# A decode step with staged caches: other landing estimates, one more staging buffer, and dependencies counted in the prompt's softmax

## The chip, the core and the metric

The kernel runs on one core of a Trainium2 chip. Five engines run their own instruction streams in program order: TensorE (PE in the profile, its weight loads PEld), VectorE (DVE), ScalarE (ACT), GpSimd (POOL) and SyncE (SP). SP issues most transfers from device memory, POOL issues the weights' transfers, some others and the gathers by index. The metric is device time in microseconds (us); three runs of the kernel before gave 618.64, 620.51 and 622.23, median 620.51.

## The reference

One layer of a decoder is computed for a prompt of 256 tokens and, at once, for 8 decode sequences of 4 new tokens with 2048 past tokens each (32 tokens), together 288 columns. In float32:

```python
h = rms_norm(x, norm_g)
c_h, c_b, c_c, c_g, q, n_g, b_g, kv6, m_q, m_g = split_cols(h @ w_in)
y_a, conv_new = short_conv_mixer(c_h, c_b, c_c, conv_prev, w_conv)      # short gated convolution
...
o_cmp, o_sel = nsa_cmp_sel(q, q_rot, pos, k_cmp, v_cmp, k_sel, v_sel)   # compressed and selected keys
o_win = gqa_attend(q_rot, win_k, win_v, wmask)                          # sliding window of 512
o_m = gqa_attend(m_q, mem_k, mem_v, None)                               # 256 memory tokens
mixed = concat([y_a, gated(o_cmp, o_sel, o_win), gated(o_m)])
y = rms_norm(x + mixed @ w_out, final_g)
```

Past keys and values lie in a pool of pages, found by a page table; there are compressed keys and values (means weighted by `a_cmp` over 64 rows), selected keys and values, a window cache and a memory cache. The memory keys and values of the prompt are projected from `mem_prompt`. Besides `y` the step returns new rows of all caches.

## The kernel before, in words

**Products.** All projections are done as tiles of 128 output channels by 288 (or 256) columns. A weight tile of 128 x 2048 is loaded in two halves of 512 KB. Float32 accuracy comes from a split: ScalarE rounds a half to a high part `wh` (`w_hi`, L222), VectorE makes the low part `wl` (`w_lo`, L227), and `product_half` (L244) issues 24 products per half: high by high, high by low, low by high. There are 152 halves: 16 of memory, 104 of the input projection, 32 of the output projection. At product 21 of half s the load of half s + 6 is issued; at the start of half s the high part of half s + 2 and the low part of half s + 1 are made. Weight loads go through POOL from half 14 on.

**Work between the products.** Attention, softmaxes, convolution and cache handling are Python generators. After every 12 products `chunk` (L159) advances a counter `now` and lets each live generator emit its next piece. So the order on every engine is fixed when the kernel is built. A planner keeps estimated clocks while it emits: `at[0]` for PE, `at[1]` for the transfers, `at[2]` (VEC) and `at[3]` (ACT) for VectorE and ScalarE, `at[4]` (SYNC) for SP's issuing. `until(i, margin)` (L144) holds a generator until PE's clock has passed the clock of engine i (with AHEAD, until 1.5 us before). `behind(i, j)` (L140) raises clock i to clock j where an instruction on engine i needs a result of engine j. The clocks place instructions; on the chip the semaphores decide.

**Staging.** The decode caches are read in 160 pieces of 512 KB into staging buffers of 128 x 1024: `buffers` holds six (L721). `loads` lists the pieces in the order of their due times. `load_next` (L725) hands each free buffer the next piece, and `loading` (L151) estimates when it has landed: the transfer clock plus `DMA_PIECE` per piece (weights count in the same clock), or SP's issuing clock if that is later, plus `DMA_LAG`. `stage_stream` (L740) uses the stages in order and waits, in chunks, until its pieces are there by the estimate. A stage of compressed pages (`cmp_use`, L344; 64 of them) takes one piece: VectorE and POOL multiply a half each, VectorE sums (`pooled`). The other stages take four pieces and are products of 32 columns on PE: selected and window keys (`sk`), memory keys (`memk_use`, L614, tile `smd`), selected and window values (`od`), memory values (`omd`). `used_up` (L736) returns the buffers and asks for the next loads. A seventh buffer, the prompt's memory queries `mq`, joins in `prompt_mems` (L1321) when the prompt's memory attention is done; it is part of a tile named `qk` in the profile. The decode memory queries lie in `qmz`, 128 x 4 x 2 x 4 x 32, read last by the second memory-key stage. Where `stage_stream` has to wait, PE is given products meanwhile.

**The prompt.** `prompt_all` runs `prompt_cmp` (L1216: scores against four compressed blocks, their softmax in `pc`, weights `pc3`) and then four times `prompt_nsa` (L1268), each of which transposes a part of `pc3` first (`pct`). `split_y1` (L1382) makes the operands of the first eight tiles of the output projection (`y1a`, `y1b`) when the prompt is done and the decode memory answer has come; `split_decode` (L1420) waits for both halves of the decode answer.

Of the kernel before, what the change touches and what calls it, by code (L numbers as in the profile page):

```python
# [50 lines left out]
WAIT, AHEAD = 0.8, -1.5  # L51
# [5 lines left out]
T_WIN = (20, 31)  # L57
T_LAST = 4
LAST_PASS = 272
DMA_PIECE, DMA_LAG = 1.75, 4.0  # L60
CMP_GAP = 1.75
ISSUE = {"cmp_load": 1.5, "selk_load": 3.75, "selv_load": 0.0}
EARLY = 154
# [14 lines left out]
def decode_step(ctx, tc, xT, xN, xD, memT, cst, w_in, w_mem, w_out, w_bg, pt, ptv, ckc, ckk, ckv, wk, wv, mk, mv,  # L78
# [17 lines left out]
    now = [0]  # L96
# [3 lines left out]
    at = [6.0, 6.0, 6.0, 6.0, 6.0]  # L100
    VEC, ACT, SYNC = 2, 3, 4
# [8 lines left out]
    def matmul(out, a, b, **kw):  # L110
        n = size(out)
        k, t = ((0, n / 2400 + 0.0115) if b.dtype == F32R else (1, n * 0.00048 + 0.008) if out.shape[0] == 32
                else (2, max(0.21, n * 0.00143)))
        if k != kind[0]:
            at[0] += 0.2 if 1 in (k, kind[0]) else 0.08
        kind[0] = k
        at[0] += t
        nc.tensor.matmul(out, a, b, **kw)  # L118

    def transpose(out, a, b):  # L120
        kind[0] = 2
        at[0] += 0.107
        nc.tensor.transpose(out, a, b)  # L123
# [16 lines left out]
    def behind(i, j):  # L140

        at[i] = max(at[i], at[j])

    def until(i, margin=WAIT):  # L144

        t = at[i]
        yield 1
        while at[0] < t + margin:
            yield 1

    def loading(us, issue=0.0):  # L151
        at[1] = max(at[1], at[0]) + us
        at[SYNC] = max(at[SYNC], at[0]) + issue
        return max(at[1], at[SYNC]) + DMA_LAG

    def spawn(gen, delay=0):
        live.append([now[0] + delay, gen])
# [22 lines left out]
    def small(w, name, bufs=2):  # L180
        return psm.tile([128, w], F32, name=name, tag=name, bufs=bufs)
# [5 lines left out]
    c = one.tile([128, CW], F32, name="cst")  # L187
# [3 lines left out]
    def C(name):  # L191
        o, w = _COFF[name]
        return c[:, o:o + w]
# [21 lines left out]
    def w_load(s):  # L215
        if s < NH:
            raws[s] = pw.tile([128, 1024], F32, name=f"w{s}", tag="wr", bufs=WR)
            if s > 1:
                (nc.gpsimd if s >= ON_SYNC else nc.sync).dma_start(raws[s], wsrc[s])  # L219
            loading(DMA_PIECE)  # L220
# [96 lines left out]
    qmz = one.tile([128, 4, 2, 4, 32], F32, name="qmz")  # L317
# [296 lines left out]
    def memk_use(j, t):  # L614
        if j == 0:
            assert "o" not in env
            env["o"] = 1
            env["mo"] = pos.tile([128, 512], F32, name="smd", tag="o")
        s = env["mo"]
        for h, x in enumerate(t):  # L620
            tv = x.rearrange("p (c s) -> p c s", c=4)
            for c_ in range(4):
                matmul(s[32 * c_:32 * c_ + 32, j * 256:(j + 1) * 256], qmz[:, c_, j, h, :], tv[:, c_], start=(h == 0), stop=(h == 3),
                       skip_group_check=True)
        if j == 1:
            spawn(mem_softmax(), 1)
        return
        yield

    def mem_softmax():  # L630
        s = env["mo"]
        env.pop("o")
        vec.tensor_tensor(Sm, s.rearrange("p (b s) -> p b s", b=2), C("memadd").unsqueeze(2).to_broadcast([128, 2, 256]),
                                op=ALU.add)
        Sv = Sm.rearrange("p b s -> p (b s)")
        mx, nm, sm = small(1, "mx1"), small(1, "nm1"), small(1, "sm1")
        vec.tensor_reduce(mx, Sv, axis=AX.X, op=ALU.max)
        vec.tensor_scalar(nm, mx, -SCALE, None, op0=ALU.mult)
        yield from until(VEC, AHEAD)
        behind(ACT, VEC)  # L640
        act.activation(Sv, Sv, AF.Exp, scale=SCALE, bias=nm, accum_out=sm)
        yield 1
        behind(VEC, ACT)
        vec.reciprocal(sm, sm)
        behind(ACT, VEC)
        act.activation(Sv, Sv, AF.Copy, scale=sm)
        yield from until(ACT)
        t = ptr.tile([128, 512], F32, name="ptmd", tag="t")
        for j in range(4):
            transpose(t[:, j * 128:(j + 1) * 128], Sv[:, j * 128:(j + 1) * 128], ident)  # L650
        act.activation(Sv, t, AF.Copy)
        env["mem_weights"] = True
# [69 lines left out]
    free = []  # L722
    nl = [0]

    def load_next():  # L725

        while nl[0] < len(loads) and free:
            f, u, j, n = loads[nl[0]]
            t = free.pop(0)
            f(j, n, t)  # L730
            tiles_of.setdefault((u, j), []).append(t)
            place.setdefault((u, j), []).append(t)
            ready[u, j] = loading(DMA_PIECE, ISSUE.get(f.__name__, 0.6))
            nl[0] += 1
# [481 lines left out]
    def prompt_cmp():  # L1216
        rows = pbig.tile([128, 1024], F32, name="vrows", tag="big")[:, :192].rearrange("p (g r h n) -> p g r h n", g=2, r=3, h=8)
        vec.memset(rows, 0.0)
        for g in range(2):
            vec.tensor_copy(rows[:, g, :, 4 * g:4 * g + 4, :],  # L1220
                                  pool_p[:, 1, g].unsqueeze(1).unsqueeze(1).to_broadcast([128, 3, 4, 4]))
        yield from until(VEC)
        t = ptr.tile([128, 512], F32, name="kcps", tag="t")
        matmul(t[:, 0:8], wcmp[:, 0], pool_p[:, 0].rearrange("p g n -> p (g n)"), start=True, stop=True)
        for g in range(2):
            matmul(t[0:96, 128 + g * 128:256 + g * 128], rows[:, g].rearrange("p r h n -> p (r h n)"), wcmp[:, 1], start=True, stop=True)
        nc.gpsimd.memset(kcp, 0.0)
        vec.tensor_copy(kcp[:, :, 0:4], t[:, 0:8].rearrange("p (g n) -> p g n", g=2))
        v = vcp.rearrange("p g d -> p (g d)")
        act.activation(v, t[0:96, 128:384], AF.Copy)  # L1230
        vec.tensor_tensor(v[32:64], t[32:64, 128:384], v[32:64].bitcast(F32), op=ALU.subtract)
        yield from until(VEC)

        s = pss.tile([128, 512], F32, name="scp", tag="s")
        for i in range(4):
            matmul(s[32 * i:32 * i + 32, :], kcp[:, i // 2, :], qq[:, 2 * i:2 * i + 2, :].rearrange("p h t -> p (h t)"), start=True,
                   stop=True, skip_group_check=True)
        sT = pbig.tile([128, 1024], F32, name="scpT", tag="big")
        act.activation(sT[:, :512], s, AF.Copy)
        yield from until(ACT)  # L1240
        t = ptr.tile([128, 512], F32, name="scpt", tag="t")
        for i in range(4):
            transpose(t[:, i * 128:(i + 1) * 128], sT[:, i * 128:(i + 1) * 128], ident)
        add = C("cmpadd").rearrange("p (a n) -> p a n", a=2)
        m01 = C("cmp01").rearrange("p (a n) -> p a n", a=2)
        tv = t.rearrange("p (h a i n) -> p a i h n", h=2, a=2, i=4)
        for a in range(2):
            vec.tensor_tensor(pc[:, a].rearrange("p (i h) n -> p i h n", h=2), tv[:, a, :, :, 0:4],
                                    add[:, a].unsqueeze(1).unsqueeze(1).to_broadcast([128, 4, 2, 4]), op=ALU.add)
        mx, sm = small(16, "mxc", 1), small(16, "smc", 1)  # L1250
        pcv = pc.rearrange("p a h n -> p (a h) n")
        bc = lambda x: x.unsqueeze(2).to_broadcast([128, 16, 4])
        vec.tensor_reduce(mx, pcv, axis=AX.X, op=ALU.max)
        vec.tensor_tensor(pcv, pcv, bc(mx), op=ALU.subtract)
        yield 1
        act.activation(pcv, pcv, AF.Exp, scale=SCALE)
        yield 1
        vec.tensor_reduce(sm, pcv, axis=AX.X, op=ALU.add)
        vec.reciprocal(sm, sm)
        smv = sm.rearrange("p (a h) -> p a h", a=2)  # L1260
        vec.tensor_tensor(smv, smv, gp[:, :, :, 0], op=ALU.mult)
        vec.tensor_tensor(pc, pc, m01.unsqueeze(2).to_broadcast([128, 2, 8, 4]), op=ALU.mult)
        for a in range(2):
            vec.tensor_tensor(pc3[:, a], pc[:, a].unsqueeze(1).to_broadcast([128, 3, 8, 4]),
                                    smv[:, a].unsqueeze(1).unsqueeze(3).to_broadcast([128, 3, 8, 4]), op=ALU.mult)
        yield from until(VEC)
# [62 lines left out]
    def prompt_all():  # L1329
        while not env.get("prompt_mem"):  # L1330
            yield 1
        yield from prompt_cmp()
        for g in range(2):
            for tt in range(2):
                yield from prompt_nsa(g, tt)
                yield 1
        env["prompt_done"] = True
# [159 lines left out]
    n = 0  # L1497
# [125 lines left out]
```

## Time and profile before

| what | us |
|---|---|
| three runs, median | 620.51 |
| the profiled execution | 619.23 |
| its span, first to last instruction | 616.4 |
| TensorE busy | 600.2 (97%) |
| VectorE busy | 458.6 (74%) |
| ScalarE busy | 285.9 (46%) |
| GpSimd busy | 200.4 (33%) |
| transferred | 188.40 MB, 306 GB/s on average |

The profile comes from one execution, so durations are compared with its own 619.23 us: the span and 2.83 us around it. An engine's busy time is the union of its instructions; matrix multiplies overlap, so PE's busy share isn't its share of peak. A row of the waits says which engine's instruction stood idle, at which line, and what released it. In the order of time a row has its start, its duration, engine, line, operation, `out<-in`, count, and in brackets the idle time ahead of it with what ended it. Nearly all matrix work has the line of one helper (L118), all VectorE and ScalarE work that of another (L135), so groups go by the names of tiles: `z` are the projections, `st` the staging buffers, `wh` and `wl` the parts of a weight half.

### The profile page before, as it was taken

Reading aid. Unit: us, or ns where it says so; the run is one execution under the profiler, and the core shown is the slowest. Engines: PE = TensorE matmul, PEld = TensorE weight load, DVE = VectorE, ACT = ScalarE, POOL = GpSimd, SP = SyncE. Lnnn points to the kernel's source line nnn. Section 1 sums busy time; section 2 is a strip of 40 time slices with the busy share of each in tenths; the row PEclk is TensorE's granted clock in tenths of the full one; section 3 lists DMA queues with packets and bytes.
Section 4 is the critical chain, followed back from the end, with each engine's and each line's share of the span. In section 5 each row is a group of like instructions: output and inputs, shape, how many; then the busy total and the mean of one; then the engine's idle time right before and its main releaser. Section 6 shows DMA issues by size and latency. Waiting matters only on the chain.

```text
span 616.4 us, 13330 instructions
## 1 busy us (share of the span) xinstructions
PE 600.2 (97%) x4893; PEld 557.9 (91%) x4893; DVE 458.6 (74%) x737; ACT 285.9 (46%) x500; POOL 200.4 (33%) x282
## 2 busy tenths in 40 slices
PE   8999999999999999999999999999999999999993
PEld 5998999989999899978998989888898898999993
DVE  5789899978477499988987879897568633357754
ACT  4855545544364345325434434353445444346650
POOL 2022545434234242323464523331212364122300
PEclk9999999999999999999999999999999999999997
DMA  8999898999888998897898998989898889677723
GB/s 313 407 403 402 261 328 314 319 312 368 310 287 303 362 388 309 295 385 267 295 316 260 318 366 288 297 283 332 303 355 321 337 285 312 225 253 276 234 86 153
DMA packets 74929, 188.40 MB, mean 306 GB/s; under 512 B 8752, under 2 KB 26064, under 8 KB 74608
## 3 DMA queue, kind: packets, MB, share of 16 engines
q0 software_dynamic: 26048, 100.48, 46.3%
q1 hardware_dynamic: 47664, 85.11, 39.0%
q10 hardware_dynamic: 1152, 1.97, 0.9%
q8 instruction: 38, 0.62, 0.4%
q14 instruction: 27, 0.22, 0.1%
HBM read 182.31 MB, written 13.60 MB: 318 GB/s over the span
## 4 chain that ended last, share of the span: by engine, by line
PE 82%; DVE 8%; DMA 6%; issue 2%; SPq 1%; ACTq 0%; ACT 0%; DVEq 0%
PE z L118 64%; PE od L118 3%; PE sk L118 3%; DMA st<-ckc 2%; PE zf L118 2%; DVE pooled L135 2%; DMA st<-ckk 2%; PE acc L118 2%; DVE wl L135 2%; PE s L118 2%; DMA qk<-ckk 1%; DMA mraw<-memT 1%; PE pt L123 1%; DVE st L135 1%; DVE ysum L135 1%
## 5 line engine op out<-in xcount | busy, mean ns | idle before, releaser
L118 PE MATMUL z<-x,wh 128*128 128x288 f32 x1664 | 254.5, 302 | 0.0
L135 DVE TENSOR_TENSOR wl<-w,wh 128x1024 fp32r<-128x1024 f32 x148 | 185.1, 1252 | 85.4 <-PE z L118 43.2
L118 PEld LDWEIGHTS z<-x,wh 128*128 128x128 f32 x1664 | 229.8, 188 | 7.8 <-issue 6.1
L135 ACT ACTIVATE wh<-w 128x1024 fp32r<-128x1024 f32 x148 | 154.4, 1052 | 19.1 <-PE z L118 14.5
L118 PE MATMUL z<-x,wl 128*128 128x288 f32 x832 | 127.0, 295 | 0.3 <-DVE wl L135 0.3
L118 PEld LDWEIGHTS z<-x,wl 128*128 128x128 f32 x832 | 115.8, 188 | 0.6 <-DVE wl L135 0.6
L350 POOL TENSOR_TENSOR st<-st,cst 128x512 f32<-128x512 f32 x63 | 69.3, 1102 | 131.5 <-DVE st L135 53.3
L219 POOL DMA_DIRECT2D w<-w_in x104 | 58.3, 560 | 109.3 <-DVE wl L135 79.2
L135 DVE TENSOR_REDUCE pooled<-st 128x16 f32<-128x1024 f32 x63 | 76.3, 1210 | 5.8 <-POOL st L350 5.8
L135 DVE TENSOR_TENSOR st<-st,cst 128x512 f32<-128x512 f32 x63 | 43.0, 684 | 10.6 <-DMA st<-ckc 10.5
L219 POOL DMA_DIRECT2D w<-w_out x32 | 17.5, 551 | 63.1 <-DVE wl L135 42.3
L578 POOL DMA_INDIRECT st<-ckv,rows_v x26 | 27.0, 1037 | 33.9 <-PE od L118 18.9
L118 PE MATMUL z<-y,wh 128*128 128x288 f32 x256 | 37.0, 297 | 0.0
L118 PE MATMUL z<-y1a,wh 128*128 128x288 f32 x224 | 35.4, 298 | 0.0
L118 PEld LDWEIGHTS z<-y,wh 128*128 128x128 f32 x256 | 35.1, 188 | 0.0
L118 PEld LDWEIGHTS z<-y1a,wh 128*128 128x128 f32 x224 | 31.4, 188 | 2.1 <-issue 1.2
L118 PE MATMUL z<-m,wh 128*128 128x256 f32 x192 | 27.3, 287 | 0.5 <-DVE mvt L135 0.5
L135 ACT ACTIVATE P<-P,nm 128x128 f32<-128x128 f32 (+1 forms) x32 | 14.2, 445 | 27.9 <-DVE nm L135 27.9
L118 PEld LDWEIGHTS z<-m,wh 128*128 128x128 f32 x192 | 24.7, 191 | 0.8 <-issue 0.7
L135 ACT ACTIVATE ysum<-z 128x288 f32<-128x288 f32 x16 | 6.6, 412 | 35.2 <-PE z L118 35.2
L118 PE MATMUL z<-y,wl 128*128 128x288 f32 x128 | 19.6, 295 | 0.0
L118 PE MATMUL sk<-st,qz 128*32 128x256 f32 x272 | 19.6, 383 | 0.0
(286 smaller groups left out, 691.6 us busy)
## 6 DMA issues: line engine op xcount, KB each, us to landing
w<-w_in POOLq DMA_DIRECT2D x104, 512.0 KB, 6.0
st<-ckc SPq DMA_DIRECT2D x126, 256.0 KB, 5.6
w<-w_out POOLq DMA_DIRECT2D x32, 512.0 KB, 5.1
st<-ckk SPq DMA_DIRECT2D x112, 128.0 KB, 4.6
w<-w_mem SPq DMA_DIRECT2D x13, 512.0 KB, 7.6
o_wk<-wk POOLq DMA_DIRECT2D x8, 512.0 KB, 6.1
o_wv<-wv POOLq DMA_DIRECT2D x8, 512.0 KB, 6.5
st<-mv SPq DMA_DIRECT2D x7, 512.0 KB, 6.5
```

What stands on the lines that cost most here:

```text
L118: nc.tensor.matmul(out, a, b, **kw)
L123: nc.tensor.transpose(out, a, b)
L135: return getattr(self.engine, name)(*args, **kw)
L219: (nc.gpsimd if s >= ON_SYNC else nc.sync).dma_start(raws[s], wsrc[s])
L350: done.append(eng.tensor_tensor(tm[:, :, kv], tm[:, :, kv], acmp[:, kv].unsqueeze(1).unsqueeze(1).to_broadcast([128, 2, 4, 64]), op=ALU.mu ...
L578: nc.gpsimd.indirect_dma_start(t, None, ckv, bass.IndirectOffsetOnAxis(ap=rows_v[:, j * 4 + b:j * 4 + b + 1], axis=0))
```

## The change

```diff
-DMA_PIECE, DMA_LAG = 1.75, 4.0
+DMA_PIECE, DMA_LAG, LATER = 1.6, (7.5, 6.0), 165
...
     def loading(us, issue=0.0):
         at[1] = max(at[1], at[0]) + us
         at[SYNC] = max(at[SYNC], at[0]) + issue
-        return max(at[1], at[SYNC]) + DMA_LAG
+        return max(at[1], at[SYNC]) + DMA_LAG[now[0] >= LATER]
...
         if j == 1:
             spawn(mem_softmax(), 1)
+            free.append(qmz.rearrange("p c b h n -> p (c b h n)"))
+            load_next()
...
         act.activation(v, t[0:96, 128:384], AF.Copy)
+        behind(VEC, ACT)
         vec.tensor_tensor(v[32:64], t[32:64, 128:384], v[32:64].bitcast(F32), op=ALU.subtract)
...
         vec.tensor_tensor(pcv, pcv, bc(mx), op=ALU.subtract)
-        yield 1
+        yield from until(VEC, AHEAD)
+        behind(ACT, VEC)
         act.activation(pcv, pcv, AF.Exp, scale=SCALE)
         yield 1
+        behind(VEC, ACT)
         vec.tensor_reduce(sm, pcv, axis=AX.X, op=ALU.add)
```

The transfer clock counts 1.6 instead of 1.75 us for each piece of 512 KB. The lag from there to the landing is 7.5 us before chunk 165 and 6.0 from then on, instead of 4.0 throughout. After the second stage of memory keys the tile `qmz` is appended to the free buffers, as an eighth, and the next load is asked for at once. In `prompt_cmp` the clock of VectorE is raised to ScalarE's after the copy of the compressed values (`vcp`) and after the exponentials, ScalarE's to VectorE's before them, and the exponentials wait until PE's clock is at most 1.5 us short of VectorE's. No computation is added, removed or altered; the order in which pieces are emitted follows from the new clocks.

## The prediction

> **What bounds the kernel now.** I read the page first, then the waits of TensorE stretch by stretch, then the instructions around each wait in order of time, and last the stretches and the chain. The page:
>
> ```profile
> span 616.4 us, 13330 instructions
> ...
> PE 600.2 (97%) x4893; PEld 557.9 (91%) x4893; DVE 458.6 (74%) x737; ACT 285.9 (46%) x500; POOL 200.4 (33%) x282
> ...
> GB/s 313 407 403 402 261 328 314 319 312 368 310 287 303 362 388 309 295 385 267 295 316 260 318 366 288 297 283 332 303 355 321 337 285 312 225 253 276 234 86 153
> ```
>
> TensorE (PE) is busy 97% of the span, and the edits add or remove no matrix multiply. So the change can win only what PE now waits, and lose only by new waits. The waits of PE alone, from 125 to 280 us (engine, line, what it waited for; total, times, longest):
>
> ```profile
> PE pct L123 <- DVE pc L135: 1.2, 1, 1.2
> PE sk L118 <- DMA qk<-ckk: 0.7, 1, 0.7
> PE acc L118 <- DVE pcT L135: 0.3, 1, 0.3
> PE z L118 <- DVE wl L135: 0.3, 1, 0.3
> PE scp L118 <- DVE kcp L135: 0.3, 1, 0.3
> ```
>
> The same view has no row from 60 to 125 us and none from 280 to 601 us. So 2.8 us is all that can be won in the middle; the first 60 us and the output at the end are not touched by any edit.
>
> Where they come from, in order of time (start, duration, [idle before <- what ended it]); first PE:
>
> ```profile
> 211.75 0.38 PE L118 MATMUL sk<-qk,qz 128*32 128x256 f32 x1 [0.69 <-DMA qk<-ckk]
> 259.73 1.07 PE L118 MATMUL scp<-qq,kcp 128*32 128x512 f32 x8 [0.26 <-DVE kcp L135]
> 272.73 0.28 PE L123 MATMUL pct<-cst,pc 128*96 128x128 f32 x1 [1.24 <-DVE pc L135]
> 276.54 0.50 PE L118 MATMUL acc<-pcT,vcp 96*128 96x512 f32 x1 [0.29 <-DVE pcT L135]
> ```
>
> Then VectorE (DVE), which works in program order, so that everything behind a waiting instruction waits too:
>
> ```profile
> 215.15 0.69 DVE L135 TENSOR_TENSOR st<-st,cst 128x512 f32<-128x512 f32 x1 [6.23 <-DMA st<-ckc]
> 260.12 0.42 DVE L135 TENSOR_TENSOR vcp<-kcps,vcp 32x256 fp32r<-32x256 f32 x1 [0.45 <-ACT vcp L135]
> 267.37 0.69 DVE L135 TENSOR_TENSOR st<-st,cst 128x512 f32<-128x512 f32 x1 [0.76 <-DMA st<-ckc]
> 269.70 0.69 DVE L135 TENSOR_TENSOR st<-st,cst 128x512 f32<-128x512 f32 x1 [1.64 <-DMA st<-ckc]
> 271.44 0.21 DVE L135 TENSOR_REDUCE smc<-pc 128x16 f32<-128x64 f32 x1
> ```
>
> and its waits for staged pages in the same stretch:
>
> ```profile
> DVE st L135 <- DMA st<-ckc: 10.5, 5, 6.2
> ```
>
> Five times DVE stood before a staged page that the planner had counted as landed. The last two holds, 0.76 + 1.64 = 2.40 us, lie just ahead of the prompt's softmax sum at 271.44, and PE's 1.24 us wait for that softmax's result ends at 272.73. So 0.7 (keys) and 1.5 (softmax and what follows it) of the 2.8 us are late pages. The 0.3 us on wl has no DMA wait ahead of it.
>
> **Part 1, the new estimates.** The planner counts a load ready at its DMA clock plus the piece plus the lag (L151 to L154). The lag rises by 3.5 us before chunk 165 and by 2.0 after; the piece falls by 0.15 us for each load queued in that clock. Following the planner's arithmetic through the old kernel, its DMA clock runs at most 12 us ahead, 12 / 1.75 = 7 pieces, so an estimate rises by at least 3.5 - 7 x 0.15 = 2.45 us early, and 2.0 - 1.05 = 0.95 late. Nothing is issued that was not issued before; uses of staged tiles move later against the matrix products, and loads behind them move with the buffers.
>
> - The keys' wait: late by 0.69, estimate up by 2.45 or more, so the use is placed behind the landing. Bounds 0 to 0.7 gained; I take 0.7.
> - Softmax and acc: DVE's hold was 2.40 against 2.45. Bounds 0 to 1.5; that is a bare cover and the order around it will differ, so I take 1.0.
> - The wl wait: bounds 0 to 0.3; taken as 0, because DVE is the late one there, not a page.
>
> What is queued behind a page that is now asked for differently is SP's own order. SP issues most staged loads and stands for buffers in between (start, duration of the stretch of issues):
>
> ```profile
> 134.85 14.24 SPq L336 DMA_DIRECT2D st<-ckk  x16
> 202.28 3.17 SPq L336 DMA_DIRECT2D qk<-ckk  x4
> 252.39 14.70 SPq L336 DMA_DIRECT2D st<-ckc  x8
> ```
>
> A tile freed later delays all loads behind it on SP; the larger lag holds each tile longer, so this part alone slows staging. The smaller piece works the other way: in the planner's arithmetic the DMA clock is idle for only 1.4 us in all between 61 and 535 us, so the piece is what paces staging, and 1.75 / 1.6 = 1.094 times the pace is what it now asks. Stretches (busy us of each engine, clock, DMA share, GB/s):
>
> ```profile
> 125.00:220.00 95.00, 94.03 (x781) 88.91 (x781) 65.86 (x86) 43.50 (x80) 34.95 (x50) 1.00 0.94 328
> 220.00:280.00 60.00, 58.21 (x517) 53.43 (x516) 54.92 (x109) 22.52 (x35) 19.11 (x29) 1.00 0.93 343
> 280.00:360.00 80.00, 80.00 (x636) 71.81 (x635) 66.69 (x99) 35.67 (x72) 40.30 (x47) 1.00 0.86 295
> 360.00:440.00 80.00, 80.00 (x638) 72.19 (x637) 64.60 (x102) 35.20 (x73) 21.99 (x31) 1.00 0.92 307
> ```
>
> All waits lie where the DMA share is 0.93 to 0.94; at 0.86 to 0.92 there are none. Times 1.094 the last two become 0.94 and 1.01. What new waits cost there is not in the trace. Lower bound 0 (the rows from 280 on as they are). Upper bound: the density of 125 to 280, 2.8 / 155 = 0.018 us per us, over 280 to 470 (the planner's DMA clock would end its staging some 65 us earlier than its 532): 190 x 0.018 = 3.4 us. I take 0.5, near the lower end, since the landings there start from a better place. Median time to landing, 125 to 280 us:
>
> ```profile
> st<-ckc SPq DMA_DIRECT2D x48, 256.0 KB, 7.0
> w<-w_in POOLq DMA_DIRECT2D x39, 512.0 KB, 6.5
> ```
>
> and 280 to 440 us:
>
> ```profile
> st<-ckc SPq DMA_DIRECT2D x38, 256.0 KB, 5.5
> w<-w_in POOLq DMA_DIRECT2D x36, 512.0 KB, 5.7
> ```
>
> Weights are covered: a half is asked for at the end of one half product and converted three halves later, 3 x 24 x 0.132 = 9.5 us (a dozen products take 1.58, below), against 6.5. If landings pass 9.5, ScalarE's conversion and then PE wait by the excess. DVE's share for staged pages:
>
> ```profile
> L135 DVE TENSOR_REDUCE pooled<-st 128x16 f32<-128x1024 f32 x63 | 76.3, 1210 | 5.8 <-POOL st L350 5.8
> ```
>
> 63 tiles over the 378 us or so in which they are used are 27 in 160 us; 9% more is 2.4, at 0.69 + 1.21 us each 4.6 us on top of 66.69 + 64.60 = 131.3 us from 280 to 440: 0.85 busy, under the 0.92 that DVE shows from 220 to 280. If it weren't so, wl would be late for PE.
>
> **Part 2, one more buffer.** After the second memory-key stage (last use near 266 us) the queries' tile takes loads. The load behind it goes to SP, which must then wait for PE's 32 small products (1.86 us, as the od row below), and SP stands still until 267.1 anyway. No load is added, each comes earlier. PE gains nothing by it directly: 0; what it does to the pace is in part 1.
>
> **Part 3, the softmax dependencies.** The 0.45 us of DVE on ACT's vcp was not counted, and PE met kcp 0.26 us early. Counted, the score products come a dozen products later or not at all. Bounds 0 to 0.3; I take 0.2. Its cost is at most two dozens of products of delay in the prompt's chain, PE being filled meanwhile. The cover, from the chain and from the tile of split activations:
>
> ```profile
> 417.70 1.58 PE z L118 x12
> 435.88 1.72 PE acc L118 x4
> 474.02 1.86 PE omd L118 x32
> 532.93 1.86 PE od L118 x32
> 538.28 62.34 PE z L118 x468
> ...
> L118 PE MATMUL z<-y1a,wh x224: 288/295/402, 486.2 to 549.5; 128*128 128x288 f32 x112
> L135 DVE TENSOR_TENSOR y1a<-mixed,y1a x7: 224/447/459, 442.0 to 484.5; 128x288 fp32r<-128x288 f32 x4, 128x256 fp32r<-128x256 f32 x2, 128x64 fp32r<-128x64 f32 x1
> ```
>
> The prompt's last product is at 437.6 and its first reader at 486.2, so 3.2 us cost nothing. The memory answer is nearer: the last split starts 1.7 us before its reader.
>
> **The sum.** -0.7 - 1.0 - 0.2 + 0.5 = -1.4 us. The profiled execution took 619.23 (span 616.4 and 2.83 around it); it becomes 617.8. It lies 1.28 below the median of the runs shown, 620.51; against that median I predict 619.1.
>
> **Rivals.**
> Staging outruns the DMA (slower). It decides once the DMA share from 280 on passes 0.93, and its price is the upper bound with nothing won: 620.5 + 3.4 = 623.9. For it: 0.92 x 1.094 = 1.01, and five holds at 0.93 to 0.94. Against it: bigger lag, one buffer more, and slices at 385 and 388 GB/s, while a 512 KB piece every 1.6 us is 328. The Trainium skill, "DMA: Bandwidth & Descriptors", section "Specifications", puts the HBM limit of one core near 358 GB/s; by it the asked pace plus the outputs would sit close under the limit and this rival's 623.9 would be the time. The trace agrees only in part: the first slices show 407, 403 and 402 GB/s.
>
> The memory answer comes late (slower). If the extra buffer brings nothing, each late stage waits 2.0 - 0.15 = 1.85 us longer; three of them (window keys, two memory-value stages) are 5.6, less the 1.7 of margin: 3.9, 624.4. Against it: seven buffers hold one four-piece stage and only three pieces of the next, eight hold two.
>
> Every wait goes (faster): 620.51 - 2.8 = 617.7, and down to 617.7 - 1.28 = 616.4 if such waits are also what sets the median above the profiled execution. Against it: wl.
>
> Nothing moves on balance: waits change places, the 0.5 is nearer 1.9: 620.5.
>
> **Chances.** Forecast 0.46; every wait goes 0.13; no balance 0.17; DMA outrun 0.16; memory answer late 0.08. About 0.5%, 3.1 us, is what a measurement of this kernel tells from no change. Faster by more (below 617.4): half of the case in which every wait goes, 0.07, and 0.11 out of the forecast by the spread of the runs (618.64 to 622.23): 0.18. Slower by more (above 623.6): 0.13 and 0.07 of the two slower rivals, 0.20. Within: 0.62. The range runs from 616.4 (all waits and the median's excess) to 623.9 (DMA outrun).
>
> **What would show it.** Right: no DMA wait ahead of sk, and DVE's waits for ckc well under 10 us in the stretch 125 to 280; pct without its 1.2 us; staged loads ended near 470 us instead of 523; DMA share from 280 to 440 above 0.9 and lower after. Part 3: vcp without idle time before it. Wrong: rows of waits for PE after 280 us, a wl wait grown, a y1a reader waiting, or 2.8 us gone and the time the same, which would mean that PE's waits are not what sets the end.

## The result and the profile after

The changed kernel is slower: 625.1 us median (624.61 to 629.08, four runs) against 619.58 (617.17 to 622.23, four runs) of the kernel before, ratio 1.0114 with the 95% interval 1.0072 to 1.0157. The forecast was 619.1 with a range of 616.4 to 623.9; it has the wrong sign and the time lies outside the range. The loss is clear of the noise, at little over one per cent. The profiled execution took 625.54 us against 619.23, and its span is 7.4 us longer. The first lines of the page after:

```profile
span 623.8 us, 13337 instructions
...
PE 602.5 (97%) x4893; PEld 558.0 (89%) x4893; DVE 458.7 (74%) x737; ACT 286.6 (46%) x500; POOL 203.7 (33%) x282
```

Every engine has nearly the work it had. The 3552 projection products are the same, too, and from the start of the first to the start of the last they take 589.2 us instead of 582.0; ahead of them it has 20.9 us instead of 20.7, behind them the same 13.6. So all 7.2 us lie inside, where the prediction had 2.8 us of waits to win. The waits of TensorE from 60 to 605 us (engine, line, what it waited for; total, times, longest):

```profile
PE pt L123 <- DVE P L135: 1.7, 1, 1.7
PE pe L123 <- DVE odr L135: 1.7, 1, 1.7
PE od L118 <- DMA st<-ckv,rows_v: 1.3, 1, 1.3
PE otm L123 <- DVE odr L135: 0.8, 1, 0.8
PE sm L118 <- ACT S L135: 0.8, 1, 0.8
PE scp L118 <- DVE kcp L135: 0.6, 1, 0.6
PE sc L118 <- ACT S L135: 0.4, 1, 0.4
PE z L118 <- DVE wl L135: 0.3, 1, 0.3
PE acc L118 <- DVE pcT L135: 0.2, 1, 0.2
PE sk L118 <- DMA st<-wk: 0.2, 1, 0.2
```

The keys' 0.7 us for `qk<-ckk` and the softmax's 1.2 us for `pc` are gone, as forecast. In their place stand ten rows, 8.0 us where before had 3.0 (the 2.8 that the prediction shows, and 0.2 for `ssqy` at 603.9, which after lies past 605). Most of it is TensorE waiting for an operand that VectorE or ScalarE has not made yet (5.3 and 1.2 us); 1.5 us are transfers. The same waits in the order of time (start, duration, [idle ahead <- what ended it]):

```profile
167.78 0.48 PE L118 MATMUL sm<-mixed,qk 128*128 128x256 f32 x1 [0.80 <-ACT S L135]
272.21 0.30 PE L123 MATMUL pe<-cst,odr 128*128 128x128 f32 x1 [1.69 <-DVE odr L135]
313.35 0.63 PE L123 MATMUL pt<-cst,P 128*128 128x128 f32 x4 [1.73 <-DVE P L135]
361.14 1.16 PE L118 MATMUL od<-st,S 128*32 128x256 f32 x6
363.64 1.91 PE L118 MATMUL od<-st,S 128*32 128x256 f32 x26 [1.33 <-DMA st<-ckv,rows_v]
446.06 0.33 PE L118 MATMUL sc<-kcT,qz 128*32 128x32 f32 x16 [0.42 <-ACT S L135]
471.94 0.30 PE L123 MATMUL otm<-cst,odr 128*128 128x128 f32 x1 [0.84 <-DVE odr L135]
```

A wait costs more than its row says, since products ahead of it stretch: the 32 products of the stage at 361.14 reach to 363.64 + 1.91 - 0.07 = 365.48, the start of the next products, 4.34 us instead of the 1.86 of such a stage, 2.5 more for a row of 1.3. So for each kernel I also summed, from the starts of TensorE's products, how much longer than its usual step each run of like products took (only excesses over 0.45 us, 60 to 600 us). Before this sum is 3.4 us, after 11.1; the 7.7 between them account for the 7.2. It is called "lost" below. What counts as the usual step is a choice: other choices move single sums by up to 2.2 us, so differences of that size between kernels say nothing. Of the 11.1 us, 2.5 lie at this one stage of transfers; most of the rest lies ahead of operands of VectorE and ScalarE.

Apart from that stage the transfers are not what got worse. VectorE's waits for compressed pages from 125 to 280 us fell from 10.5 us to

```profile
DVE st L135 <- DMA st<-ckc: 3.9, 3, 3.2
```

and the transfer engines are hardly busier (stretch, length, busy us of each engine, clock, DMA share, GB/s):

```profile
280.00:360.00 80.00, 78.03 (x624) 70.27 (x624) 66.71 (x98) 30.50 (x59) 42.78 (x47) 1.00 0.89 320
360.00:440.00 80.00, 78.67 (x619) 69.90 (x618) 64.70 (x103) 34.82 (x71) 21.79 (x30) 1.00 0.92 319
```

against 0.86 and 0.92 before. TensorE was busy in all 80 us of both stretches before, and now it isn't.

The one transfer that is late shows best what the estimates did. It is the fourth stage of selected values, gathered through POOL. Before, POOL's last gather and the stage's first product:

```profile
352.28 0.94 POOL L578 DMA_INDIRECT qk<-ckv,rows_v  x1 [0.30 <-issue]
```
```profile
364.03 0.42 PE L118 MATMUL od<-st,S 128*32 128x256 f32 x3
```

After, on POOL, with what stood between its gathers, and the chain of waits for the last one:

```profile
345.87 1.98 POOL L578 DMA_INDIRECT st<-ckv,rows_v  x1 [5.18 <-DVE qk L135]
...
348.91 1.14 POOL L350 TENSOR_TENSOR qk<-qk,cst 128x512 f32<-128x512 f32 x1
...
353.45 0.94 POOL L578 DMA_INDIRECT st<-ckv,rows_v  x1 [0.30 <-issue]
```
```profile
353.45 10.15 DMA st<-ckv,rows_v
```

Before, the use stood 11.75 us behind the start of the last gather; after, 7.69 (361.14 - 353.45), and the gather took 10.15. It had taken 8.55 before, so it became slower as well; the old distance would still have covered 10.15. The estimate that was to rise put this use 4 us nearer to its load.

### The profile page after: what moved, and what is told of

Its sections match the earlier page's. It is cut to its first block, busy times and chain, and to the rows that moved or that the text cites. A ratio compares the mean times of both kernels' runs of the same rounds, so it can differ in the third digit from the quotient of the medians.

```text
span 623.8 us, 13337 instructions
## 1 busy us (share of the span) xinstructions
PE 602.5 (97%) x4893; PEld 558.0 (89%) x4893; DVE 458.7 (74%) x737; ACT 286.6 (46%) x500; POOL 203.7 (33%) x282
## 4 chain that ended last, share of the span: by engine, by line
PE 45%; DVE 6%; DMA 3%; issue 2%; POOL 1%; SPq 0%; ACT 0%; DVEq 0%; POOLq 0%
PE z L118 35%; PE od L118 3%; DMA st<-wk 2%; DMA st<-ckv,rows_v 2%; PE acc L118 1%; PE s L118 1%; PE sk L118 1%; DVE pooled L135 1%; DVE wl L135 1%; PE pt L123 1%; DVE ysum L135 1%; DVE st L135 1%; PE pv L123 1%; PE omd L118 1%; DVE P L135 0%
## 5 line engine op out<-in xcount | busy, mean ns | idle before, releaser
L135 DVE TENSOR_TENSOR wl<-w,wh 128x1024 fp32r<-128x1024 f32 x148 | 181.1, 1224 | 89.4 <-PE z L118 40.6
L118 PE MATMUL z<-x,wl 128*128 128x288 f32 x832 | 126.9, 295 | 0.3 <-DVE wl L135 0.3
L350 POOL TENSOR_TENSOR st<-st,cst 128x512 f32<-128x512 f32 x56 | 61.9, 1107 | 115.3 <-issue 54.7
L135 DVE TENSOR_REDUCE pooled<-st 128x16 f32<-128x1024 f32 x56 | 67.8, 1211 | 6.6 <-POOL st L350 6.6
L578 POOL DMA_INDIRECT st<-ckv,rows_v x25 | 28.4, 1137 | 41.6 <-PE od L118 13.5
L118 PE MATMUL od<-st,S 128*32 128x256 f32 x240 | 19.2, 383 | 1.3 <-DMA st<-ckv,rows_v 1.3
L135 ACT ACTIVATE se<-z 128x288 f32<-128x288 f32 x16 | 6.5, 406 | 29.8 <-PE z L118 29.8
```

The source lines that it names most:

```text
L135: return getattr(self.engine, name)(*args, **kw)
L350: done.append(eng.tensor_tensor(tm[:, :, kv], tm[:, :, kv], acmp[:, kv].unsqueeze(1).unsqueeze(1).to_broadcast([128, 2, 4, 64]), op=ALU.mu ...
L578: nc.gpsimd.indirect_dma_start(t, None, ckv, bass.IndirectOffsetOnAxis(ap=rows_v[:, j * 4 + b:j * 4 + b + 1], axis=0))
```

## The experiments

18 kernels were run. Their ratio is to the kernel before on the same chip, with a 95% interval; "stretch" is the time from the first to the last projection product and "lost" the sum defined above, both of the one profiled execution.

| kernel | ratio | median us | stretch | lost |
|---|---|---|---|---|
| before | 1 | 617.7 to 619.6 | 582.0 | 3.4 |
| changed | 1.0114 (1.0072 to 1.0157) | 625.1 | 589.2 | 11.1 |
| e1 estimates alone | 1.0188 (1.0148 to 1.0227) | 630.33 | 592.8 | 15.2 |
| e2 buffer alone | 1.0096 (1.0067 to 1.0125) | 625.95 | 588.5 | 9.2 |
| e4 both, no softmax | 1.0148 (1.0114 to 1.0182) | 627.71 | 591.4 | 14.0 |
| e8 changed, lags 8.0 and 6.5 | 1.0103 (1.0062 to 1.0145) | 624.64 | 587.3 | 8.0 |
| n1 before, lag 3.75 | 1.0072 (1.0041 to 1.0104) | 623.62 | 584.8 | 6.1 |
| n2 before, lag 4.5 | 1.0023 (0.9989 to 1.0056) | 621.57 | 586.3 | 8.2 |
| p1 changed, no GpSimd half | 0.9996 (0.9964 to 1.0028) | 619.77 | 583.0 | 5.1 |
| p2 before, no GpSimd half | 0.9961 (0.9932 to 0.9989) | 616.47 | 578.4 | 0.9 |
| r1 changed, half on VectorE | 1.0077 (1.0053 to 1.0101) | 624.79 | 588.9 | 10.8 |
| r2 before, half on VectorE | 1.0058 (1.0028 to 1.0088) | 622.66 | 583.7 | 5.1 |
| u1 changed, one use a chunk | 1.0032 (1.0013 to 1.0051) | 620.76 | 583.9 | 4.8 |
| u2 before, one use a chunk | 1.0027 (0.9993 to 1.0061) | 619.94 | 587.3 | 8.6 |
| g4 changed, piece 1.55 | 1.0177 (1.0135 to 1.0220) | 629.9 | 593.3 | 15.1 |
| g2 changed, piece 1.65 | 1.0126 (1.0084 to 1.0167) | 626.16 | 589.1 | 10.6 |
| g3 changed, piece 1.70 | 1.0043 (1.0024 to 1.0061) | 620.52 | 584.0 | 5.9 |
| g1 changed, piece 1.75 | 1.0001 (0.9971 to 1.0032) | 619.51 | 582.0 | 3.3 |
| h1 piece 1.70, one use a chunk | 1.0054 (1.0030 to 1.0079) | 622.48 | 585.8 | 7.3 |
| h2 piece 1.75, lags 7.0 and 5.5 | 1.0033 (1.0003 to 1.0063) | 621.19 | 583.5 | 3.6 |

In all 20 rows the stretch less the lost time is 577.4 to 579.9 us. So within 2.5 us each kernel's stretch is that of the same products plus what they lose beside waits, whatever was edited. The profiled execution of u2 was 5.4 us above its median, those of r2 and n1 2.8 and 2.4 below, so the two last columns are not typical of these three.

**The parts alone.** e1 takes only the estimates, e2 only the buffer, e4 both without the softmax lines. The two softmax dependencies alone leave the planned order as it was before, so no run shows them by themselves.

```diff
 e1: -DMA_PIECE, DMA_LAG = 1.75, 4.0
     +DMA_PIECE, DMA_LAG, LATER = 1.6, (7.5, 6.0), 165
     (and DMA_LAG[now[0] >= LATER] in loading)
 e2: +free.append(qmz.rearrange("p c b h n -> p (c b h n)"))
     +load_next()
 e4: e1 and e2
```

> The new piece and lags alone: no eighth buffer, no softmax dependencies. In the planner's own arithmetic the last staged use moves from 532 to 543 us, the split that the output projection needs comes six chunks after it is needed, and the planner spends 6 idle steps of 1.4 us there, so that its PE clock ends 8.7 us later (602.2 to 610.9). If the planner's clock is a fair picture of the end, the time is 620 + 8.7 = about 628, with PE waiting for the operand y1a near 486 to 495 us. If waits that come by chance of the order decide (theory C), the memory answer has margin on the chip and the time scatters within 616 to 626. If late landings decide (theory B), 622 to 626 with DMA waits ahead of sk and od.

> The eighth buffer alone, with the old piece and lag. Planned latency of a load is 13.7 us before chunk 165 and 15.3 after it, against 13.0 and 13.0 of the kernel before, and 13 uses fall into the chunk of the use before, against 12 before and 17 in the changed kernel. Theory A (uses that follow each other in one chunk meet tiles of PSUM and results of VectorE that are not free yet) and theory B (pages land late because the DMA clock was drained) both expect no slower than before: 617 to 620, PE waits from 125 to 601 us at 2 to 4 us. Theory C (any new order brings its own chance waits) expects 620 to 626 here as well, with waits of 5 us or more in places that neither theory names.

> The changed kernel without the three counted dependencies and the extra wait in the prompt's softmax. By its planner 18 uses fall into the chunk of the use before and the planned latency is that of the changed kernel (13.5 and 13.1 us). Theories A and B expect the changed kernel's time, 624 to 626, with a DMA wait ahead of od and waits of PE for S and odr. Theory C expects another set of waits: anything from 617 to 627. If the dependencies did the harm, 619 to 621.

Measured: 1.0188, 1.0096 and 1.0148. Neither the estimates nor the buffer is harmless alone, and the three together measured less than the estimates alone (the intervals just meet). In e1 the longest wait of TensorE from 60 to 605 us is for the memory answer's operand:

```profile
PE otm L123 <- DVE odr L135: 4.3, 1, 4.3
PE acc L118 <- DVE pcT L135: 2.0, 1, 2.0
PE pe L123 <- DVE odr L135: 1.7, 1, 1.7
PE pct L123 <- DVE pc L135: 1.3, 1, 1.3
```

This is the rival of the late memory answer: with the larger lag and no eighth buffer, the planner itself has six steps without a product before the output projection, and its own end moves from 602.2 to 610.9. The eighth buffer takes that away (e4, 601.9 by the planner), so in the changed kernel this rival is not what happened. e2, with the old estimates, shows the keys met early, and VectorE late for the memory answer. Theories A and B had expected 617 to 620, C 620 to 626, so its 625.95 us speaks for C:

```profile
PE otm L123 <- DVE odr L135: 2.5, 1, 2.5
PE sk L118 <- DMA st<-ckk: 1.4, 1, 1.4
PE sk L118 <- DMA qk<-ckk: 1.3, 1, 1.3
```

Without the dependencies (e4) `scp` waits 0.6 us for `kcp`, and with them 0.6 as well. The intervals of e4 and the changed kernel overlap; whether the dependencies bring anything is not shown.

**Is the lag the wrong size?** e8 raises both lags of the changed kernel by 0.5; n1 and n2 move the old lag by small steps.

```diff
 e8: +DMA_PIECE, DMA_LAG, LATER = 1.6, (8.0, 6.5), 165
 n1: +DMA_PIECE, DMA_LAG = 1.75, 3.75
 n2: +DMA_PIECE, DMA_LAG = 1.75, 4.5
```

> The changed kernel with both lags half a microsecond larger (8.0 and 6.5). Nothing else differs. Theories A and B expect a little less than the changed kernel, 623 to 625.5, the same places of waiting (odr near 272 us, P near 312 us, gathered values near 363 us). Theory C expects different places and a time that can differ from the changed kernel's by 3 us either way: 618 to 628.

> The kernel before with one number moved a little the other way: lag 3.75 instead of 4.0; piece, buffers and softmax as before. By the planner's own arithmetic nothing is worse: no idle step, its PE clock ends at 602.2 as before, the prompt is done one chunk later, the memory answer two. Stretch from the first to the last projection product: 582.0 us before, 589.2 changed. Theory A/B (the particular edits do the harm, by bunching or late landing) expects 582 to 583.5 here, time 619 to 620.5. Theory C (the order before is one that fits, and most other orders cost waits of PE on VectorE's results) expects 585 to 590, time 622 to 627.

> The kernel before with lag 4.5 instead of 4.0: half a microsecond of more caution for landings, nothing else. The planner sees no idle step and an end at 602.1. If late landings were what cost time before (DMA waits of 0.7 us and the softmax's waits behind late pages), the stretch between first and last projection product falls from 582.0 to 580 to 582, time 617 to 619. Theory C expects 585 to 590, time 622 to 627.

Measured: 1.0103, 1.0072, 1.0023. Half a microsecond more does not mend the changed kernel. And a quarter of a microsecond less in the old kernel costs 0.7%: the old constants sit at a good place, and a small step from it gives another order with other waits. This sets the grain of every comparison here: single differences of 0.3 to 0.7% between two orders can be the draw, that is, the luck of the order, and not the reason given for the edit.

**The piece.** In the changed kernel with nothing else altered, the piece goes from 1.55 to 1.75.

```diff
 g4: +DMA_PIECE, DMA_LAG, LATER = 1.55, (7.5, 6.0), 165
 g2: +DMA_PIECE, DMA_LAG, LATER = 1.65, (7.5, 6.0), 165
 g3: +DMA_PIECE, DMA_LAG, LATER = 1.70, (7.5, 6.0), 165
 g1: +DMA_PIECE, DMA_LAG, LATER = 1.75, (7.5, 6.0), 165
```

> The changed kernel with the old piece of 1.75 us (lags, buffer and softmax dependencies as changed). With it the planner's DMA clock keeps running ahead, 5.1 and 6.7 us at a load on average before and after chunk 165, where the changed kernel has 3.4 and 3.8 (before the change: 7.1 and 6.3), so that a load is planned 15.0 us from its issue to its use, against 13.6 and 13.5 changed and 13.0 before. Theory B (the smaller piece takes back what the larger lag gives, and landings come late) expects no DMA wait ahead of od or sk, and 619 to 622. Theory C expects 621 to 627 with waits on VectorE's results.

> The changed kernel with a piece of 1.70 us. Planned time from issue to use 14.4 and 14.5 us, 16 uses bunched. Theory B expects a time between those of 1.65 and 1.75: 1.003 to 1.008. Theory C expects any ratio from 0.998 to 1.015.

> The changed kernel with a piece of 1.65 us. Planned time from issue to use: 13.8 us before chunk 165 and 13.7 after it (1.6: 13.6 and 13.5; 1.75: 15.0 and 15.0); 17 uses bunched in a chunk, as with 1.6. Theory B (the piece sets how much time the planner leaves a load and how closely uses follow each other) expects close to the changed kernel, 1.008 to 1.012 of the kernel before. Theory C (orders are good or bad by chance) expects any ratio from 0.998 to 1.015.

> The changed kernel with a piece of 1.55 us. Planned time from issue to use 13.4 and 13.1 us, 17 uses bunched, no idle step of the planner. Theory B expects the changed kernel's time or more: 1.010 to 1.018. Theory C expects any ratio from 0.998 to 1.015.

Measured, from 1.55 up: 1.0177, 1.0114 (the change itself), 1.0126, 1.0043, 1.0001. The time falls with a larger piece, 1.60 and 1.65 being alike within their intervals. Theory B had g1, g3 and g4 right and g2 a little too low (1.012 at most); theory C missed g1 (621 to 627 us) and g4 (1.015 at most). With the old piece the rest of the change, taken together, costs nothing that can be measured. The waits of TensorE from 60 to 605 us, with 1.75:

```profile
PE scp L118 <- DVE kcp L135: 1.4, 1, 1.4
PE pt L123 <- DVE P L135: 1.0, 1, 1.0
PE z L118 <- DVE wl L135: 0.3, 1, 0.3
PE ssqy L118 <- ACT ysq L135: 0.2, 1, 0.2
```

and with 1.55 four of the largest:

```profile
PE acc L118 <- DVE pcT L135: 3.7, 2, 3.2
PE od L118 <- DMA st<-ckv,rows_v: 1.4, 2, 0.8
PE pt L123 <- DVE P L135: 1.1, 1, 1.1
PE pct L123 <- DVE pc L135: 1.1, 1, 1.1
```

The gathered values' wait (`od`) is 1.4 us at 1.55, 1.3 at 1.60 and 0.2 at 1.65, and there is none at 1.70 and 1.75; the rest is operands of VectorE and ScalarE, a few of them in every order (`wl`), most in some orders only. The planner's own arithmetic goes the same way. Its transfer clock ran on average 7.1 us (chunks 70 to 165) and 6.3 us (165 to 240) ahead of TensorE's when a load was asked for in the kernel before, 3.4 and 3.8 in the changed one, 5.1 and 6.7 with the piece of 1.75. Add piece and lag, and the time from load to landing that it plans is 13.0 and 13.0 before, 13.6 and 13.5 after, 15.0 and 15.0 with 1.75.

**Uses that fall into one chunk.** The planner put 17 staged uses of the changed kernel into the chunk of the use before, 12 of the old one. Two stages in a row then ask VectorE and ScalarE for their softmax work at once. u1 and u2 let a chunk pass behind each use; h1 does so at a piece of 1.70; h2 keeps 1.75 with other lags, which gives 12 such uses as in the old kernel.

```diff
 u1, u2, h1:
             if u is not cmp_use:
                 used_up(u, j)
+                yield 1
 h1: +DMA_PIECE, DMA_LAG, LATER = 1.7, (7.5, 6.0), 165
 h2: +DMA_PIECE, DMA_LAG, LATER = 1.75, (7.0, 5.5), 165
```

> The changed kernel with one more chunk after each use that goes to PE, so that no two uses fall into one chunk (17 do in the changed kernel, 12 in the one before, here 0). The planner sees no idle step and an end at 602.7. Theory A (bunched uses make PE wait for PSUM tiles and VectorE's results) expects PE's waits between 60 and 605 us from 8.0 to 3 to 4 us and a time of 619 to 621. Theory C expects a new set of waits, 621 to 627.

> The kernel before with one more chunk after each use that goes to PE (1 use falls into the chunk of another, instead of 12): control for the same edit of the changed kernel, which took it from 1.0114 to 1.0032, and a candidate for better than both. Theory A (bunching costs wherever it occurs) expects a gain of some of the 3.0 us of PE's waits: 0.995 to 1.000. Theory C expects 1.002 to 1.010, as for the other small moves of the kernel before.

> The changed kernel with a piece of 1.70 us instead of 1.60, and at most one staged use in a chunk. With 1.70 alone (g3) the ratio to the kernel before was 1.0043, and at 1.60 the spreading of the uses (u1) took the ratio from 1.0114 to 1.0032, 0.8%. Theory A (uses that fall into one chunk make TensorE meet VectorE's results unready): what 1.70 cost goes, ratio 0.998 to 1.002, and TensorE's waits for VectorE from 60 to 605 us fall below the 2.7 us of g3. Theory B (the order is merely a different draw, and spreading helped by luck at 1.60): ratio 1.002 to 1.010, waits 3 to 6 us.

> The changed kernel with the old piece of 1.75 us and lags of 7.0 and 5.5 us instead of 7.5 and 6.0: by the planner's arithmetic 12 uses fall into the chunk of the use before, as in the kernel before (14 in g1, 17 in the changed kernel), and the planned time from issue to use is 14.7 and 14.8 us. Theory A (piece and bunching decide): as g1 or better, ratio 0.995 to 1.001, waits of TensorE from 60 to 605 us 1 to 3 us. Theory C (every order but the one that the old constants give costs about a per cent, and g1 was a lucky one): ratio 1.004 to 1.010, waits 4 to 7 us.

Measured: u1 1.0032, so spreading takes back 0.8 of the 1.1%, its waits of TensorE are 3.6 us in all and `od` isn't among them. But u2 is 1.0027, h1 1.0054 against 1.0043 without spreading, and h2 1.0033 with fewer such uses than g1, which has 14 and 1.0001. So shared chunks are not the cause as such: where they were removed at another piece nothing was won. What u1 showed is that the order of the changed kernel is bad in places that a delay of one chunk mends. Neither h1 nor h2 beats the kernel before.

**The granted clock.** Some of the losses are not waits themselves. In four of the traces TensorE's granted clock is half for 3.4 us inside the stretch: e1 (from 368.8 and from 495.1 us), g4 (323.9), n2 (306.4) and u2 (159.3). Each time TensorE stood idle then or just before, for 1.5 to 4.3 us. In e1 (PE, then the stretch with its clock, 0.50, before the last two numbers):

```profile
495.75 0.48 PE L123 MATMUL otm<-cst,odr 128*128 128x128 f32 x1 [4.27 <-DVE odr L135]
```
```profile
495.10:498.50 3.40, 2.75 (x12) 2.75 (x13) 1.41 (x6) 1.54 (x3) 0.76 (x2) 0.50 1.02 399
```

It does not follow every such wait: the 1.7 us in the changed kernel and 2.5 us in e2 and g2 left the clock at 1.00. As an estimate from these figures, 3.4 us at half the clock cost at most 1.7 us: 3.4 for the two of e1 and 1.7 for g4, that is up to 0.5 and 0.3 of their 1.9 and 1.8%. The traces of before, changed and g1 to g3 have no such drop inside the stretch, so it explains neither the change's loss nor the return to 1.0001.

**GpSimd beside VectorE.** At 313.35 TensorE waits 1.73 us for the prompt's softmax, and VectorE had been held on it. VectorE's row and POOL's after:

```profile
310.97 2.23 DVE L135 TENSOR_TENSOR P<-P,sm 128x512 f32<-128x512 f32 x1
```
```profile
310.33 1.19 POOL L578 DMA_INDIRECT st<-ckv,rows_v  x1 [2.78 <-DVE pooled L135]
311.54 1.10 POOL L350 TENSOR_TENSOR st<-st,cst 128x512 f32<-128x512 f32 x1
```

p1 and p2 leave GpSimd's multiplication of half of each compressed page out of both kernels, with its instruction order otherwise kept; that part of the computation is missing. r1 and r2 let VectorE do that half from page 20 on. The dependency that holds GpSimd's half behind VectorE's goes with it.

```diff
 p1, p2: +for kv, eng in ((0, vec),):
 r1, r2: +for kv, eng in ((0, vec), (1, nc.vector if s >= 20 else nc.gpsimd)):
```

> The changed kernel without GpSimd's multiplication of half of each compressed page (the compressed values are summed unweighted, so this part of the computation is left out; 64 instructions of about 1.1 us on GpSimd). Order and loads stay. Theory D (VectorE is held by GpSimd's multiplications: VectorE's P at 310.97 took 2.23 instead of 0.69 us while GpSimd multiplied, and PE waited 1.7 us for it) expects PE's waits on VectorE to fall from 5.3 to under 2 us and the stretch from 589.2 to 584 to 586, time 619 to 622. If only the order matters, the waits stay: 588 to 590, time 624 to 626.

> The kernel before without GpSimd's multiplication (same part left out), the control of the run above: what GpSimd's multiplications cost where the order fits. Theory D expects little, since they met only weight halves made ahead of need (2.07 and 2.66 instead of 1.23 us): 581 to 582 for the stretch, time 618 to 620, so that the gain is larger in the changed kernel by 2 us or more. If GpSimd costs the same in both, both fall by the same amount.

> The changed kernel, with GpSimd's half of the multiplication done by VectorE from compressed page 20 on (44 instructions of about 0.6 us more on VectorE, as many of 1.1 us fewer on GpSimd) and the planner left ignorant of it, so that the order of everything else stays. Nothing is left out of the computation. Theory D (VectorE held by GpSimd's multiplications) expects most of what leaving the half out gave, 7 us by the intervals: the stretch of projections from 589.2 to 584 to 587, time 619 to 622, no VectorE instruction of 512 columns that takes over 1.3 us. If the gain there came only from less work on GpSimd and VectorE's waits for it, the 26 us more on VectorE put the softmax chains later and the time is 624 to 628.

> The same in the kernel before, order unchanged: control of the run above and a candidate for better than both. Leaving the half out altogether gave 2.4 us here. Theory D: 581 to 583 for the stretch, time 617.5 to 619.5 (gain by no holds, against 0.6 us more per page on VectorE). If VectorE's work counts instead: 584 to 587, time 621 to 625.

Measured: without those multiplications the changed kernel falls from 1.0114 to 0.9996, 1.18% or 7.3 us, the old one by 0.39% or 2.4 us. So 4.9 us of the loss, by the intervals some 1 to 9, need GpSimd's multiplications in the new order. It does not show by which of their effects: they hold VectorE, they make VectorE's sums wait, and they stand between gathers on POOL. Moving them (r1) makes the ratio 0.37% smaller, which the intervals do not tell from nothing, and costs the old kernel 0.58%, where VectorE then has the work itself. Theory D, that the holds are what cost, had the time of p1 right; but TensorE's waits for VectorE are 3.0 us there, not under 2. For r1 it had 619 to 622 and missed: 624.8 lies with the rival, VectorE's added work. The products of two inputs that VectorE took too long for add up to 5.0 us before and 6.8 after, by their excess over the usual 0.69 and 1.23; in r1 there is none. So the holds alone are not shown to make the loss. In r1 the gathered values are still late:

```profile
PE od L118 <- DMA st<-ckv,rows_v: 1.7, 2, 1.3
```

So the multiplication at 348.91 on POOL was not by itself what made them so; the last section shows what stands there in its place. r1 does not beat the kernel before either.

**What is settled, and what is open.** In the changed kernel the loss goes with the piece: with 1.75 alone put back it is gone. It is paid as time that TensorE loses ahead of operands of VectorE and ScalarE and of one gathered stage. Open stays how much of the 1.1% follows from the shorter lead as such and how much is this order's draw. The kernels that share a piece differ by as much as the whole loss: from 1.0032 (u1) to 1.0188 (e1) at 1.60, and at 1.75 from 1.0001 (g1) over 1.0033 (h2) and 1.0072 (n1) to 1.0096 (e2). Nor does the planned time from load to landing put them in order: e2 plans 13.7 and 15.3 us, more than the kernel before, and loses 1.0%; u1 plans 12.9 and 12.9 us by the planner's arithmetic, less than the changed kernel, and loses 0.3%. No run changes the piece alone in the old kernel.

## Why the prediction was wrong, step by step

- **The waits that would go.** Right for the two that were named. No row of `sk` for `qk<-ckk` and none of `pct` is left, which is the 0.7 and the 1.2 of the sum. The 0.3 of `acc` at 276.5 is gone, too; the 0.2 of `acc` that is there now belongs to the second of the prompt's four parts, at 325.7. `wl` keeps its 0.3, as said.
- **The softmax dependencies, -0.2.** Wrong. With the old constants they move nothing, and in the new order `vcp` still stands 0.45 us for ScalarE, and `scp` waits 0.6 instead of 0.3:

```profile
261.26 0.42 DVE L135 TENSOR_TENSOR vcp<-kcps,vcp 32x256 fp32r<-32x256 f32 x1 [0.45 <-ACT vcp L135]
```

 What delays `kcp` is not `vcp`, which comes behind it, but a sum of a compressed page ahead of it that waits for GpSimd (VectorE, after):

```profile
259.51 1.22 DVE L135 TENSOR_REDUCE pooled<-st 128x16 f32<-128x1024 f32 x1 [0.98 <-POOL st L350]
260.65 0.17 DVE L135 COPY kcp<-kcps 128x8 f32<-128x8 f32 x1
```

- **The step that failed: "an estimate rises by at least 3.5 - 7 x 0.15 = 2.45 us early, and 2.0 - 1.05 = 0.95 late".** It held the queue of seven pieces fixed and changed only what each counts. But the queue is what the piece makes: the weights and pages are asked for by TensorE's clock, and a clock that charges less for each drains. The lead fell from 7.1 and 6.3 us to 3.4 and 3.8, so the estimates rose by 0.6 and 0.5 us on average, and some fell: that of the fourth gathered stage from 14.7 to 12.3 us, so that its use came 4 us nearer to its last gather. That the clock was idle for only 1.4 us between 61 and 535 us was taken for a sign that the piece paces the staging; with the new constants it is idle for about 45 us there. With the old piece (g1) the rise is 2.0 us in both parts, and there the kernel is not slower. This step is false in any case; that it alone made the loss is not shown (e2 and u1 above).
- **The cost of the new order, +0.5, bounds 0 to 3.4.** The second failure, and the term that the time went wrong by. The upper bound was the density of the old waits put onto the stretch from 280 on. The rows from 280 on are `pt` 1.7, `od` 1.3, `otm` 0.8, `sc` 0.4, `sk` 0.2 and `acc` 0.2, 4.6 us, over the bound. Two rows before 280 (`sm` 0.8, `pe` 1.7, together 2.5) were in no term at all, and `scp`, which was to go, doubled to 0.6: there I counted only what could go. A new order draws its waits anew over the whole kernel; e1 to n2 drew 6.1 to 15.2 us lost where before has 3.4. The cover that I named for VectorE from 280 to 440 (0.85 busy at most) held, 66.71 + 64.70 of 160 us, and TensorE still waited: the mean busy share says nothing about the microsecond in which an operand is wanted.
- **Staging outruns the DMA, 623.9.** Near the measured time, and not its mechanism: it was to decide at a DMA share over 0.93 from 280 on, forecast as 0.94 and 1.01, and the rows show 0.89 and 0.92. Nor did staging end near 470 us; the last gather starts at 519.3 instead of 523.4. The piece did not set that pace alone: SP still waits for buffers to come free, 70.5 us for VectorE's `pooled` from 60 to 540 us (126.9 before).
- **The memory answer late, 624.4.** The nearest time of all, by chance. Its mechanism is seen in e1, where the planner has steps without products, not in the changed kernel: `y1a` is complete at 481.8 us and first read at 493.7.
- **Every wait goes, and no balance.** Neither: the old ones went and others of more than twice their size came.

## What to carry to other kernels

When an estimate is a clock plus a lag, changing what the clock charges changes how far it runs ahead; follow the clock through the whole program with the new charge before adding up the estimates. In a program whose order comes from estimates, every edit of them deals all the waits anew, and if the old constants were good the likely direction is up: set the price of a new order by what whole neighbouring orders lose (here 3.3 to 15.2 us, against 3.4 of the old one, in the runs that leave nothing out), not by the waits that one can name in the present one. And put one constant back at a time: that is how the piece was found to decide in the changed kernel.

## What the runs showed of the hardware that was not expected

How much one instruction can grow beside another engine's. The product `P<-P,sm` of 128x512 has this group (of the kernel before; least, median and greatest ns):

```profile
L135 DVE TENSOR_TENSOR P<-P,sm x8: 691/1224/1471, 287.4 to 427.0; 128x512 f32<-128x512 f32 x4, 128x1024 f32<-128x1024 f32 x4
```

So it can take 0.69 us. It took 1.47 before, where a multiplication of GpSimd runs beside it, and 2.23 after, where a gather's issue and then a multiplication do. Before, VectorE and POOL:

```profile
303.13 1.47 DVE L135 TENSOR_TENSOR P<-P,sm 128x512 f32<-128x512 f32 x1
```
```profile
302.95 1.10 POOL L350 TENSOR_TENSOR st<-st,cst 128x512 f32<-128x512 f32 x1 [4.86 <-issue]
```

In both kernels it ends some 0.55 us behind GpSimd's multiplication (304.60 and 304.05; 313.20 and 312.64): by these rows it does not share, it waits for the other's end. The other traces agree: in all 20 together 39 such products of 128x512 took over 0.9 us, and 38 of them end 0.55 or 0.56 us behind a GpSimd multiplication. The kernel before has one of them, the changed one seven. It goes the other way round, too. The issues of the gathers after, and in r1, where VectorE has more products of two inputs:

```profile
L578 POOL DMA_INDIRECT st<-ckv,rows_v x25: 936/984/1976, 299.8 to 516.8; - x25
```
```profile
L579 POOL DMA_INDIRECT st<-ckv,rows_v x25: 938/984/2577, 302.1 to 516.3; - x25
```

In r1 two of the four issues of the late stage are such long ones, 2.58 us at 344.65 and 2.35 at 349.15:

```profile
344.65 2.58 POOL L579 DMA_INDIRECT st<-ckv,rows_v  x1 [6.31 <-DVE wl L135]
...
349.15 2.35 POOL L579 DMA_INDIRECT st<-ckv,rows_v  x1 [0.30 <-issue]
```

so what the multiplication left free between them came back as longer issues. It depends on who comes first. The 20 traces have 640 such issues. Of the 264 that began while VectorE was in an instruction of two inputs, 114 took over 1.3 us, of the other 376 one; the one at 347.28 before, 0.04 us ahead of a product of 1.23, took 1.00. The Trainium skill, "SBUF — State Buffer", section "SBUF: two separate sides", says that VectorE and GpSimd take the pair of ports that they share as an exclusive lock for a whole instruction, operations of VectorE with two inputs in SBUF among them when GpSimd's instruction reads SBUF; the rows agree. Over all, GpSimd's 64 multiplications cost the old kernel 2.4 us (p2) and the changed one 7.3 (p1): the same instructions in another order.
